# First chunks' normalized pairs in buffers of their own, gate weights at lower priority, and one v projection moved, in a two-layer decoder step

## The chip, the core and the metric

The kernel runs on one core of a Trainium2 chip. The metric is the device time of one execution in microseconds (us); lower is better. A measurement gives the median of several runs. Everything here is one program whose instructions are put in order, engine by engine, when it is built: a scheduler takes the code's steps with a priority each and decides which stands where in each engine's queue. At run time every engine works through its own queue strictly in that order.

## What is computed

A prompt of 2048 positions and a group of eight short samples go through two layers. Only the first layer matters here, and of it the beginning of the prompt:

```python
u = rmsnorm(h, norm_g)
proj = u @ w_in
q, k, v, gate, g_low = jnp.split(proj, [...], axis=-1)
log_a = jax.nn.log_sigmoid((g_low @ w_gate2 + b_gate)) / A_GATE_NORMALIZER
o, state = gla_recurrence(q, k, v, log_a, state0)      # per head, in chunks
o = rmsnorm(o, out_norm_g)
return (o * jax.nn.silu(gate)) @ w_out, state
```

There are four heads with 128 key columns and 512 value columns each; the gate that decides how fast the state decays comes from a projection of rank 16 (`g_low`).

## The kernel before

**Blocks and chunks.** The prompt is cut into 4 blocks of 512 positions, and each block into 4 chunks of 128. The work goes head by head and, in a head, block by block (`blocks`, line 936): 16 stretches, one for each. Every float32 operand is carried as a pair of float16 numbers, a high and a low piece, and a product takes three passes (`PASSES`): high by high, high by low, low by high.

**Normalizing the input.** `u_steps(j)` (line 374) loads block j's x in four chunks, two halves each, and calls `norm_T` (line 298) for each chunk. That squares and sums on ACT (for the first block the second half on DVE), takes the inverse root on POOL (`rsqrt`, line 183), writes the scaled high piece on ACT and the low piece on DVE into two tiles `xt` (line 310), and sends each tile by a transposing DMA from SP's queue into `uT[j]`. The tiles have the tag `ogT` with two buffers, so one chunk's pair takes both. The same tag serves the spills of the layer's output (`spill_og`, line 620).

**The start.** The program loads the first block's x and the first head's q and k weights, then calls `split_wg` (line 335), five operations on POOL that scale the low-rank gate weights and lay them out as pairs, then loads the first head's v weights (`hw[0].v.steps()`): eight pieces of 256 KB, each split on ACT and DVE. `qk_first` (line 443) projects q and k of the first block chunk by chunk as the chunks arrive; `glow` projects the low-rank gate; `logs` turns it into the running log decay `bt`. Then comes the second block's x, and the first head's gate weights.

**The first stretch.** A `weave` at line 937 issues the projections of v of the first block's four chunks and of the gate of its first chunk (`vg_steps`, line 464; 24 matmuls of 512 columns for each v or gate of a chunk), with the decay levels as fill. The levels (`level_steps`, line 484) build the matrix of decayed scores within a chunk: a diagonal and seven levels, each a few operations on DVE, ACT and POOL, twelve small matmuls into the one `lev` bank and a masked copy on DVE. `decay_steps` makes `qe`, `ke` and `Sh` from them, in tags with `NG` = 2 buffers. In the code of each block that follows, `chunk_steps(c)` (line 566) updates the state and reads it out, woven with the projections of the next chunk (line 983), and with the levels of the next block. In the first block's own stretch also block 2's x is normalized, in the second block's stretch block 3's.

**Priorities.** `behind(steps, n)` (line 174) lowers the priority of steps by n, so that the scheduler takes them only when other work is not ready. In the second block's stretch POOL also prepares rope tables (`rope_table`, line 890), through tiles that go out to memory again.

Of the kernel before, what the change touches and what calls it, by code (L numbers as in the profile page):

```python
# [10 lines left out]
F16 = mybir.dt.float16  # L11
# [8 lines left out]
P = 128  # L20
D = 1024
# [53 lines left out]
def _body(tc, nc, cp, sb, ps, dr, i, o):  # L75
    uniq = [0]

    def nm(s):
        uniq[0] += 1
        return f"{s}_{uniq[0]}"  # L80

    def T(tag, shape, dt, bufs=None):
        return sb.tile(shape, dt, tag=tag, name=nm(tag), **({} if bufs is None else {"bufs": bufs}))
# [67 lines left out]
    def weave(main, fill):  # L151

        main, fill = list(main), list(fill)
        done = 0
        for n, f in enumerate(main):
            f()
            upto = len(fill) * (n + 1) // len(main)
            for g in fill[done:upto]:
                g()
            done = upto  # L160
        for g in fill[done:]:
            g()

    def run(steps):
        for f in steps:
            f()

    def mix(a, b):

        out = []  # L170
        weave([lambda f=f: out.append(f) for f in a], [lambda f=f: out.append(f) for f in b])
        return out

    def behind(steps, n):


        def one(f):
            with tc.high_priority(offset=-n):
                f()

        return [lambda f=f: one(f) for f in steps]

    def rsqrt(ss, n, a, b, k=1, r=None):
        m = T("rs_m", [P, 8], F32, 4)
        r = T("rs_r", [P, 8], F32, 6) if r is None else r
        pool.tensor_scalar(m[:n, :k], ss, a, b, ALU.mult, ALU.add)  # L186
        pool.tensor_tensor(r[:n, :k], m[:n, :k], mhalf[:n, :k], ALU.pow)  # L187
        return r
# [106 lines left out]

        return [lambda part=todo[x : x + per]: step(part) for x in range(0, len(todo), per)], box

    def norm_T(xh, n, dst, both=False, flat=False):

        junk = T("og", [P, 512], BF16, 1)  # L300
        ss = T("ss", [P, 3], F32, 4)
        act(junk[:n], xh[0], AF.Square, accum_out=ss[:n, 0:1])
        if both:
            junk = T("S", [P, 512], F32, 1)
            dve.tensor_tensor_reduce(junk, xh[1], xh[1], 1.0, 0.0, ALU.mult, ALU.add, ss[:, 1:2])
        else:
            act(junk[:n], xh[1], AF.Square, accum_out=ss[:n, 1:2])
        dve.tensor_tensor(ss[:n, 2:3], ss[:n, 0:1], ss[:n, 1:2], ALU.add)
        r = rsqrt(ss[:n, 2:3], n, 1.0 / D / SU / SU, EPS / SU / SU)
        xt = [T("ogT", [P, D], F16, 2) for _ in range(2)]  # L310
        for half in range(2):
            cs = slice(half * 512, half * 512 + 512)
            if both is None:
                pool.tensor_scalar(xh[half], xh[half], r[:n, 0:1], None, ALU.mult)
                split((xt[0][:n, cs], xt[1][:n, cs]), xh[half], eng=pool)
            else:
                split((xt[0][:n, cs], xt[1][:n, cs]), xh[half], r[:n, 0:1])
        for hl in range(2):
            if flat:
                nc.sync.dma_start(dst(hl), xt[hl][:n])  # L320
            else:
                nc.sync.dma_start(dst(hl), xt[hl][:n], transpose=True)

    uT = [T("uT", [P, KT, 2, 512], F16, 4) for _ in range(NBL)]
# [10 lines left out]
    def split_wg():  # L335
        pool.tensor_tensor(wg_raw, wg_raw, gs_a.unsqueeze(2).to_broadcast([P, KT, RANK]), ALU.mult)
        pool.tensor_copy(wg[:, :, :RANK], wg_raw)
        pool.tensor_tensor(wg[:, :, RANK : 2 * RANK], wg_raw, wg[:, :, :RANK], ALU.subtract)
        for n in range(1, 3):
            pool.tensor_copy(wg[:, :, n * 2 * RANK : (n + 1) * 2 * RANK], wg[:, :, : 2 * RANK])  # L340
# [33 lines left out]
    def u_steps(j):  # L374
        def chunk(c):
            if j > 0:
                t = T("W", [P, D], F32, NW)
                xh = [t[:, :512], t[:, 512:]]
            else:
                xh = [T("v", [P, 512], F32, 4) if c > 1 else T(tag, [P, 512], F32, 2) for tag in ("st", "sth")]  # L380
            for half in range(2):
                nc.sync.dma_start(xh[half], i["x_prompt"][0, j * 512 + c * P : j * 512 + (c + 1) * P, half * 512 : half * 512 + 512])
            norm_T(xh, P, lambda hl: uT[j][:, :, hl, c * P : (c + 1) * P], j == 0)

        return behind([lambda c=c: chunk(c) for c in range(4)], 20 if j > 0 else 0)

# [497 lines left out]
    def some(n=2):  # L884
        out = prep[:n]
        del prep[:n]
        return out
# [18 lines left out]
    cur = Blk(0, 0, hw[0])  # L906
# [1 line left out]
    first = u_steps(0)  # L908
    qkw = [f for u in hw[0].qk for f in u.steps()]
    run([first[0]] + qkw[:2] + [first[1]] + qkw[2:] + first[2:4])  # L910
    split_wg()
    run(hw[0].v.steps())
    load_w2()
    bgate = C("bgate", [P, 2 * AH], F32)
# [6 lines left out]
    f = T("pst", [P, 7, 64], F32, 2)  # L921
# [12 lines left out]
            wo1.units[u].t = t[:, u]  # L934

    blocks = [(h, j) for h in range(AH) for j in range(NBL)]
    weave([f for c in range(4) for f in cur.vg_steps(c, (0,))] + cur.vg_steps(0, (1,)), cur.level_steps() + cur.decay_steps())
    prev_tail = []
    samp = None
    sparts = []  # L940

    for n, (h, j) in enumerate(blocks):
# [9 lines left out]
        lv = nxt.level_steps() if nxt else []  # L952
# [13 lines left out]
        if last:  # L966
            ch = [cur.chunk_steps(c) for c in range(3)]
            weave([f for c in range(1, 4) for f in cur.vg_steps(c, (0,))], ch[0] + lv[:3] + ch[1][:3] + lv[3:5] + ch[2][:3])
            run(hw[h + 1].v.steps() if h + 1 < AH else wo.steps()[4:])
            for c in range(1, 4):  # L970
                weave(cur.vg_steps(c, (1,)), (ch[c - 1][3:] if c > 1 else []) + lv[3 + c * 2 : 5 + c * 2])
            for f in ch[2][3:]:
                f()
            run(hw[h + 1].g.steps() if h + 1 < AH else wo1.steps()[8:])
        else:
            for c in range(3):
                if n == len(blocks) - 2:
                    if c == 0:
                        wo_aside()
                    more = (wo1.steps()[:8] + wo.steps()[:4])[c * 4 : c * 4 + 4]  # L980
                else:
                    more = side[c * 2 : c * 2 + 2] if n < 2 else some(PR[j])
                weave(cur.vg_steps(c + 1, (0, 1) if n else (1,)), mix(cur.chunk_steps(c) + lv[(0,3,6)[c]:(3,6,8)[c]], sparts[(0,3,7)[c]:(3,7,99)[c]]) + more)
                if j == NBL - 2 and h + 1 < AH and c == 0:
                    hw[h + 1] = head_weights(h + 1)
                    for u in hw[h + 1].qk:
                        for f in u.steps():
                            f()
            sparts = []
# [53 lines left out]
        if j == NBL - 1:  # L1043
            sparts = samp.steps()
# [4 lines left out]
        cur = nxt  # L1049
# [636 lines left out]
    for t in range(-3, NKV * NCH):  # L1686
        fill = []
        n = t + 3
        if n < NKV * NCH:
            g, c = divmod(n, NCH)  # L1690
# [59 lines left out]
    for p_ in range(NCH // 2):  # L1750
        more = []
        if p_ + 1 < NCH // 2:
            nxt = pairs[p_ + 1]
            ld, sm = [lambda x=x, nxt=nxt: nxt.load(x) for x in (2, 3, 0, 1)], nxt.sums()
            more = ld[:2] + sm[:2] + ld[2:3] + sm[2:6]
# [88 lines left out]
```

## Time and profile before

| | us |
|---|---|
| median of 3 runs | 2862.69 |
| lowest, highest | 2857.28, 2869.30 |
| the profiled execution | 2863.85 |
| its span, first to last instruction | 2862.1 |

The profile shows one execution. PE is TensorE, DVE VectorE, ACT ScalarE, POOL GpSimd, SP the engine whose queue issues most DMAs (SPq in rows). Times in it count from the span's start. A row of a timeline gives start, length, engine, line, operation, output and inputs, how many instructions were merged and, in brackets, how long the engine was idle before and what ended that.

[...] The first hundred microseconds stand out in the profile's second part: PE is at 60% in the first of 40 slices and at 80% in the second, and at 90% or more in nearly all others.

### The profile page before, as it was taken

The numbers are of one execution on the slowest core, as the hardware profiler recorded it, in microseconds if no ns is written. First come the engines' busy times: TensorE is split into PE (matmuls) and PEld (weight loads), VectorE is DVE, ScalarE is ACT, GpSimd is POOL, SyncE is SP. The second block draws the span as 40 slices with busy tenths as digits, with TensorE's granted clock in tenths as the row PEclk, the third lists the DMA queues.
The fourth block names the chain that finished last, engine by engine and source line by source line (L and its number), as shares of the span: only waits on it lengthen the run. The fifth ranks groups of instructions, "written<-read, shape, count | busy, mean of one in ns | idle before, by whom it ended". The sixth has DMA issues, their size and how long they took to land.

```text
span 2862.1 us, 51609 instructions
## 1 busy us (share of the span) xinstructions
PE 2735.9 (96%) x19070; PEld 1392.4 (49%) x19070; DVE 1845.7 (64%) x3815; ACT 1440.3 (50%) x3385; POOL 1063.6 (37%) x1471
## 2 busy tenths in 40 slices
PE   6899999999999999999899999999999999988999
PEld 3445444444454444444344555555555555543444
DVE  5767787677768775336413666677777766767653
ACT  6655665466546654333313555566666666641110
POOL 1242233222322321116405676666566556530000
PEclk9899999999999999999999999999999999999999
DMA  8351334124312533799975555866877788798651
GB/s 209 90 124 36 100 101 150 38 82 136 115 38 85 171 84 96 180 240 282 233 193 135 108 130 120 203 117 129 173 116 130 157 155 165 151 236 172 125 112 57
DMA packets 774230, 391.78 MB, mean 137 GB/s; under 512 B 629200, under 2 KB 698776, under 8 KB 773944
## 3 DMA queue, kind: packets, MB, share of 16 engines
q1 hardware_dynamic: 761016, 352.75, 54.6%
q0 software_dynamic: 10880, 35.66, 3.4%
q8 instruction: 149, 2.44, 0.4%
q14 instruction: 105, 0.86, 0.1%
q10 hardware_dynamic: 2080, 0.07, 0.0%
HBM read 138.90 MB, written 107.54 MB: 86 GB/s over the span
## 4 chain that ended last, share of the span: by engine, by line
PE 56%; DVE 12%; DMA 11%; ACT 10%; issue 6%; POOL 4%; SPq 1%; DVEq 0%; ACTq 0%; POOLq 0%
PE pj L101 33%; PE o L101 11%; PE tr L101 8%; PE kv L101 3%; ACT o L1279 2%; DMA pst<-v 2%; DVE v L198 2%; ACT v L197 2%; DMA pre<-pst 1%; PE lev L101 1%; DMA wraw<-in_a_w_in_dram 1%; DVE o L1274 1%; DVE W L198 1%; POOL ogT L195 1%; DVE lev L1274 1%
## 5 line engine op out<-in xcount | busy, mean ns | idle before, releaser
L101 PE MATMUL pj<-W,uT 128*128 128x512 f16 x5088 | 1208.1, 383 | 6.6 <-ACT qT L430 2.9
L101 PEld LDWEIGHTS <-uT 128*128 128x128 f16 x6976 | 654.7, 99 | 714.1 <-issue 40.4
L101 PE MATMUL tr<-W,uT 128*128 128x512 f16 x1536 | 365.8, 379 | 0.0
L186 POOL TENSOR_SCALAR rs_m<-ss 128x1 f32<-128x1 f32 (+3 forms) x190 | 46.1, 243 | 685.7 <-ACT og L611 234.0
L101 PEld LDWEIGHTS <-X 128*128 128x128 f16 x2744 | 185.8, 98 | 149.3 <-issue 14.7
L1279 ACT ACTIVATE o<-o,mx 128x256 f32<-128x256 f32 (+1 forms) x384 | 168.5, 439 | 168.1 <-DVE mx L1274 163.6
L1274 DVE CUSTOM_DVE_ANT_0 o<-o,madd,nsink 128x256 f32<-128x256 f32 (+1 forms) x384 | 184.0, 479 | 48.3 <-PE o L101 44.0
L101 PE MATMUL pj<-uT,W 128*128 128x512 f16 (+1 forms) x912 | 186.0, 354 | 27.0 <-DMA uT<-ogT 24.3
L198 DVE SCALAR_TENSOR_TENSOR v<-o,v 128x512 f16<-128x512 f32 (+1 forms) x192 | 128.8, 671 | 102.0 <-ACT v L197 82.0
L187 POOL TENSOR_TENSOR rs_r<-rs_m,mhalf 128x1 f32<-128x1 f32 (+2 forms) x186 | 184.8, 994 | 14.4
L101 PEld LDWEIGHTS <-W 128*128 128x128 f16 x2448 | 128.0, 98 | 113.1 <-issue 18.5
L101 PEld LDWEIGHTS <-v 128*128 128x128 f16 x976 | 95.2, 98 | 116.0 <-DMA v<-ogd 1.9
L508 POOL TENSOR_TENSOR E<-bt 128x256 f32<-128x256 f32 x96 | 73.9, 770 | 198.4 <-DVE X L195 124.8
L195 POOL TENSOR_TENSOR ogT<-og,ogT 128x512 f16<-128x512 f32 x68 | 88.0, 1295 | 154.4 <-ACT ogT L194 142.5
L101 PEld LDWEIGHTS <-sth 128*128 128x128 f16 x2080 | 111.4, 99 | 52.3 <-DMA sth<-v 12.2
L101 PEld LDWEIGHTS <-sg 128*128 128x128 f16 x800 | 78.6, 99 | 107.5 <-DMA sg<-ogd 12.3
L101 PE MATMUL o<-gl,X 128*128 128x256 f16 (+1 forms) x768 | 114.9, 273 | 5.5 <-DMA X<-qe 5.5
L197 ACT ACTIVATE v<-o 128x512 f16<-128x512 f32 (+1 forms) x192 | 111.3, 579 | 11.1 <-DMA sth<-v 7.6
L101 PE MATMUL kv<-rmask,sth 128*128 128x64 f16 x1984 | 107.0, 194 | 10.1 <-DMA sth<-v 9.2
L101 PE MATMUL kv<-rmask,pst 128*128 128x64 f16 x992 | 102.4, 194 | 9.3 <-DMA pst<-v 9.3
L1279 ACT ACTIVATE lev<-lev,mx 128x256 f32<-128x256 f32 (+1 forms) x128 | 56.5, 441 | 103.3 <-DVE mx L1274 101.2
L101 PE MATMUL pj<-W,v 128*128 128x512 f16 x448 | 104.2, 379 | 1.1 <-DMA v<-ogd 1.1
(468 smaller groups left out, 5092.5 us busy)
## 6 DMA issues: line engine op xcount, KB each, us to landing
pre<-pst POOLq DMA_DIRECT2D x72, 256.0 KB, 3.4
W<-pre SPq DMA_DIRECT2D x36, 512.0 KB
ogd<-ogT SPq DMA_DIRECT2D x68, 256.0 KB
wraw<-in_a_w_in_dram SPq DMA_DIRECT2D x64, 256.0 KB
wraw<-in_b_w_in_dram SPq DMA_DIRECT2D x64, 256.0 KB
oge<-ogT SPq DMA_DIRECT2D x64, 256.0 KB
wraw<-in_a_w_out_dram SPq DMA_DIRECT2D x32, 256.0 KB
X<-in_x_prompt_dram SPq DMA_DIRECT2D x32, 256.0 KB
```

Of the source, the lines that this page charges most:

```text
L101: return order(nc.tensor.matmul(*a, **k))
L186: pool.tensor_scalar(m[:n, :k], ss, a, b, ALU.mult, ALU.add)
L187: pool.tensor_tensor(r[:n, :k], m[:n, :k], mhalf[:n, :k], ALU.pow)
L195: eng.tensor_tensor(lo, src, hi, ALU.subtract)
L197: act(hi, src, AF.Copy, scale=sc)
L198: dve.scalar_tensor_tensor(lo, src, sc, hi, ALU.mult, ALU.subtract)
L508: pool.tensor_tensor(Ev[:, :, 0, :], ref, btv[:, :, 0, :], ALU.subtract)
L1274: dve.tensor_tensor_reduce(pm[:, z], pm[:, z], madd.rearrange("p a b -> p (a b)")[:, (2 - nk) * P :], -0.125, nsink[:, g * GRP + h : g * G ...
L1279: act(pm[:, z], pm[:, z], AF.Exp, scale=-1.0, bias=nm_[:, h : h + 1], accum_out=bx["sum"][:, h : h + 1])
```

## The change

There are three edits. The pairs of the first block's four chunks get a tag each, `ogT`, `qe`, `ke` and `Sh`, whose tiles have the same size and are first used for their own purpose later. `split_wg` runs at a priority lower by 400. And v of the first block's fourth chunk is no longer projected in the first `weave` but in the first block's stretch, with that chunk's gate.

```diff
--- before.py
+++ after.py
@@ -295,7 +295,7 @@
 
         return [lambda part=todo[x : x + per]: step(part) for x in range(0, len(todo), per)], box
 
-    def norm_T(xh, n, dst, both=False, flat=False):
+    def norm_T(xh, n, dst, both=False, flat=False, tag="ogT"):
 
         junk = T("og", [P, 512], BF16, 1)
         ss = T("ss", [P, 3], F32, 4)
@@ -307,7 +307,7 @@
             act(junk[:n], xh[1], AF.Square, accum_out=ss[:n, 1:2])
         dve.tensor_tensor(ss[:n, 2:3], ss[:n, 0:1], ss[:n, 1:2], ALU.add)
         r = rsqrt(ss[:n, 2:3], n, 1.0 / D / SU / SU, EPS / SU / SU)
-        xt = [T("ogT", [P, D], F16, 2) for _ in range(2)]
+        xt = [T(tag, [P, D], F16, 2) for _ in range(2)]
         for half in range(2):
             cs = slice(half * 512, half * 512 + 512)
             if both is None:
@@ -380,7 +380,7 @@
                 xh = [T("v", [P, 512], F32, 4) if c > 1 else T(tag, [P, 512], F32, 2) for tag in ("st", "sth")]
             for half in range(2):
                 nc.sync.dma_start(xh[half], i["x_prompt"][0, j * 512 + c * P : j * 512 + (c + 1) * P, half * 512 : half * 512 + 512])
-            norm_T(xh, P, lambda hl: uT[j][:, :, hl, c * P : (c + 1) * P], j == 0)
+            norm_T(xh, P, lambda hl: uT[j][:, :, hl, c * P : (c + 1) * P], j == 0, tag="ogT" if j > 0 else ("ogT", "qe", "ke", "Sh")[c])
 
         return behind([lambda c=c: chunk(c) for c in range(4)], 20 if j > 0 else 0)
 
@@ -908,7 +908,7 @@
     first = u_steps(0)
     qkw = [f for u in hw[0].qk for f in u.steps()]
     run([first[0]] + qkw[:2] + [first[1]] + qkw[2:] + first[2:4])
-    split_wg()
+    run(behind([split_wg], 400))
     run(hw[0].v.steps())
     load_w2()
     bgate = C("bgate", [P, 2 * AH], F32)
@@ -934,7 +934,7 @@
             wo1.units[u].t = t[:, u]
 
     blocks = [(h, j) for h in range(AH) for j in range(NBL)]
-    weave([f for c in range(4) for f in cur.vg_steps(c, (0,))] + cur.vg_steps(0, (1,)), cur.level_steps() + cur.decay_steps())
+    weave([f for c in range(3) for f in cur.vg_steps(c, (0,))] + cur.vg_steps(0, (1,)), cur.level_steps() + cur.decay_steps())
     prev_tail = []
     samp = None
     sparts = []
@@ -980,7 +980,7 @@
                     more = (wo1.steps()[:8] + wo.steps()[:4])[c * 4 : c * 4 + 4]
                 else:
                     more = side[c * 2 : c * 2 + 2] if n < 2 else some(PR[j])
-                weave(cur.vg_steps(c + 1, (0, 1) if n else (1,)), mix(cur.chunk_steps(c) + lv[(0,3,6)[c]:(3,6,8)[c]], sparts[(0,3,7)[c]:(3,7,99)[c]]) + more)
+                weave(cur.vg_steps(c + 1, (0, 1) if n or c == 2 else (1,)), mix(cur.chunk_steps(c) + lv[(0,3,6)[c]:(3,6,8)[c]], sparts[(0,3,7)[c]:(3,7,99)[c]]) + more)
                 if j == NBL - 2 and h + 1 < AH and c == 0:
                     hw[h + 1] = head_weights(h + 1)
                     for u in hw[h + 1].qk:
```

The scheduler's order changes with it on every engine, in the first three blocks of the first head; behind that the orders of all engines agree. Three places follow.

SP's queue at the start, as it was. A `wraw` is a piece of weights that comes in, a `DMA_TRANSPOSE` sends one piece of a chunk's pair (first the high, then the low one) into `uT_156`, the first block's; `ogT_256` and 257 are the second chunk's, 293 and 294 the third's, 315 and 316 the fourth's.

```order
L322 DMA_TRANSPOSE uT_156<-ogT_256 128x8x128
L322 DMA_TRANSPOSE uT_156<-ogT_257 128x8x128
L223 DMA wraw_347<-in_a_w_in_dram 128x512
L223 DMA wraw_351<-in_a_w_in_dram 128x512
L223 DMA wraw_356<-in_a_w_in_dram 128x512
L322 DMA_TRANSPOSE uT_156<-ogT_293 128x8x128
L322 DMA_TRANSPOSE uT_156<-ogT_294 128x8x128
L223 DMA wraw_360<-in_a_w_in_dram 128x512
L108 DMA pst_364<-in_a_w_gate_dram 16x512 x3
L322 DMA_TRANSPOSE uT_156<-ogT_315 128x8x128
L322 DMA_TRANSPOSE uT_156<-ogT_316 128x8x128
```

And with the change:

```order
L223 DMA wraw_338<-in_a_w_in_dram 128x512
L322 DMA_TRANSPOSE uT_156<-qe_256 128x8x128
L223 DMA wraw_342<-in_a_w_in_dram 128x512
L322 DMA_TRANSPOSE uT_156<-qe_257 128x8x128
L322 DMA_TRANSPOSE uT_156<-ke_293 128x8x128
L223 DMA wraw_347<-in_a_w_in_dram 128x512
L322 DMA_TRANSPOSE uT_156<-Sh_315 128x8x128
L322 DMA_TRANSPOSE uT_156<-ke_294 128x8x128
L322 DMA_TRANSPOSE uT_156<-Sh_316 128x8x128
L223 DMA wraw_351<-in_a_w_in_dram 128x512
L223 DMA wraw_356<-in_a_w_in_dram 128x512
L223 DMA wraw_360<-in_a_w_in_dram 128x512
```

The transfers of chunks two to four have moved together: one load of weights stands between the second chunk's last and the fourth chunk's last, where there were four, and the low-rank gate's second weights (`pst_364`) now follow all of them.

ACT at the first block's first level, before. `v_…` is a chunk's v split, `X_748` the diagonal's split and `X_778` level 0's, `E` a decay factor, and the `ogT` are the second block's chunks.

```order
L197 ACTIVATE ogT_654<-W_642,rs_r_651 128x512 x2
L197 ACTIVATE X_748<-E_746 128x512
L197 ACTIVATE v_940<-pj_869 128x512
L510 ACT_TABLE_LOAD
L510 ACTIVATE E_772<-E_772 128x512
L197 ACTIVATE ogT_674<-W_662,rs_r_671 128x512 x2
L197 ACTIVATE v_1013<-pj_943 128x512
L194 ACTIVATE X_778<-E_772 128x512
L510 ACTIVATE E_808<-E_808 128x512
```

And with the change:

```order
L197 ACTIVATE v_963<-pj_892 128x512
L197 ACTIVATE ogT_654<-W_642,rs_r_651 128x512
L197 ACTIVATE X_744<-E_742 128x512
L197 ACTIVATE ogT_654<-W_642,rs_r_651 128x512
L510 ACT_TABLE_LOAD
L510 ACTIVATE E_769<-E_769 128x512
L477 ACTIVATE sg_1030<-pj_988 128x512
L197 ACTIVATE ogT_674<-W_662,rs_r_671 128x512 x2
L194 ACTIVATE X_775<-E_769 128x512
```

There is one v split less; the third chunk's v is done ahead of the diagonal, and the first chunk's gate (`sg_1030`) has moved ahead of level 0. On PE, level 0 now stands whole ahead of the second block's q and k, where the gate of the first chunk stood.

POOL in the second block's stretch, before. `pst` are rope tables, `rs_m` and `rs_r` the two steps of an inverse root, `ogT_1860` the low piece of a spill.

```order
L897 TENSOR_TENSOR pst_2666<-pst_2666,gq 128x512
L186 TENSOR_SCALAR rs_m_1852<-ss_1850 128x1
L897 TENSOR_TENSOR pst_2673<-pst_2673,gq 128x512
L901 DMA rtd<-pst_2666 128x8x64
L187 TENSOR_TENSOR rs_r_1853<-rs_m_1852,mhalf 128x1
L901 DMA rtd<-pst_2673 128x8x64
L195 TENSOR_TENSOR ogT_1860<-og_1849,ogT_1860 128x512
L899 TENSOR_TENSOR pst_2857<-pst_2857,gq 128x8x32
L900 TENSOR_TENSOR pst_2857<-pst_2857,gq 128x8x32
L186 TENSOR_SCALAR rs_m_1959<-ss_1955 128x1
```

And with the change:

```order
L897 TENSOR_TENSOR pst_2666<-pst_2666,gq 128x512
L897 TENSOR_TENSOR pst_2673<-pst_2673,gq 128x512
L901 DMA rtd<-pst_2666 128x8x64
L901 DMA rtd<-pst_2673 128x8x64
L186 TENSOR_SCALAR rs_m_1852<-ss_1850 128x1
L187 TENSOR_TENSOR rs_r_1853<-rs_m_1852,mhalf 128x1
L899 TENSOR_TENSOR pst_2857<-pst_2857,gq 128x8x32
L900 TENSOR_TENSOR pst_2857<-pst_2857,gq 128x8x32
L899 TENSOR_TENSOR pst_2865<-pst_2865,gq 128x8x32
L900 TENSOR_TENSOR pst_2865<-pst_2865,gq 128x8x32
L901 DMA rtd<-pst_2857 128x8x64
L195 TENSOR_TENSOR ogT_1860<-og_1849,ogT_1860 128x512
```

Both rope tables now go ahead of the first root, and four operations of the next two ahead of the spill. POOL's operations up to the first block's levels, `split_wg`'s among them, stand in the order in which they stood.

## Rows read from the trace of the kernel before

**Rows 1.** The page's first part: busy time, share of the span and instructions of each engine.

```profile
PE 2735.9 (96%) x19070; PEld 1392.4 (49%) x19070; DVE 1845.7 (64%) x3815; ACT 1440.3 (50%) x3385; POOL 1063.6 (37%) x1471
```

**Rows 2.** Busy time by stretch of 100 us: engine, instructions, granted clock, DMA share, GB/s.

```profile
0.00:100.00 100.00, 71.65 (x508) 41.43 (x509) 61.80 (x120) 60.54 (x108) 20.15 (x45) 0.93 0.69 163
100.00:200.00 100.00, 88.39 (x497) 41.63 (x496) 72.34 (x136) 59.39 (x121) 42.34 (x62) 0.93 0.54 124
```

**Rows 3.** Timeline of PE, 17 to 50 us: start, length, instructions, idle time and releaser.

```profile
23.82 2.73 PE L101 MATMUL pj<-uT,W 128*128 128x128 f16 x46 [0.34 <-DMA uT<-ogT]
...
30.32 4.21 PE L101 MATMUL pj<-uT,W 128*128 128x128 f16 x48 [0.58 <-DMA uT<-ogT]
...
35.41 2.73 PE L101 MATMUL pj<-uT,W 128*128 128x128 f16 x46 [0.66 <-DMA uT<-ogT]
37.97 3.40 PE L101 MATMUL tr<-uT,ogTs 128*96 128x512 f16 x15
41.21 6.21 PE L101 MATMUL pj<-W,uT 128*128 128x512 f16 x28
```

**Rows 4.** Timeline of the other engines and of SP's queue, 8 to 34 us.

```profile
8.38 1.01 POOL L340 COPY ogTs<-ogTs 128x256 f16<-128x256 f16 x2
...
9.48 0.24 POOL L186 TENSOR_SCALAR rs_m<-ss 128x1 f32<-128x1 f32 x1
...
22.90 1.33 ACT L197 ACTIVATE ogT<-v,rs_r 128x512 f16<-128x512 f32 x2 [0.42 <-DMA uT<-ogT]
...
24.26 2.63 SPq L322 DMA_TRANSPOSE uT<-ogT  x2
...
29.53 1.33 ACT L197 ACTIVATE ogT<-v,rs_r 128x512 f16<-128x512 f32 x2 [1.81 <-DMA uT<-ogT]
...
30.89 2.62 SPq L322 DMA_TRANSPOSE uT<-ogT  x2
```

**Rows 5.** DMA queue's share, 95 to 103 us (one transfer), and a stretch of plain loads.

```profile
q1 hardware_dynamic: 1056, 0.26, 17.1%
...
40.00:47.00 7.00, 7.00 (x34) 3.25 (x33) 2.71 (x4) 2.35 (x5) 0.00 (x0) 1.00 1.02 374
```

**Rows 6.** Timeline of ACT at 47 us, and the stretch behind it.

```profile
47.15 0.63 ACT L307 ACTIVATE og<-W 128x512 bf16<-128x512 f32 x1 [3.70 <-DMA W<-in_x_prompt_dram]
...
48.00:52.00 4.00, 4.00 (x20) 1.77 (x19) 2.76 (x6) 4.00 (x9) 0.74 (x2) 1.00 0.24 67
```

**Rows 7.** Timeline of PE, 65 to 145 us; between its rows one split on DVE.

```profile
65.47 0.33 PE L101 MATMUL lev<-one_h,X 128*128 128x1 f16 x7 [2.19 <-DVE X L198]
66.06 7.03 PE L101 MATMUL pj<-W,uT 128*128 128x512 f16 x24 [0.27 <-DVE v L198]
...
69.90 0.68 DVE L198 SCALAR_TENSOR_TENSOR v<-pj,v 128x512 f16<-128x512 f32 x1
...
92.79 7.94 PE L101 MATMUL pj<-W,uT 128*128 128x512 f16 x24 [0.35 <-ACT qT L430]
...
95.00:97.00 2.00, 2.00 (x6) 0.62 (x5) 1.24 (x3) 1.98 (x4) 0.00 (x0) 0.50 0.00 0
...
136.19 0.80 PE L101 MATMUL lev<-X 128*128 128x64 f16 x12 [5.29 <-ACT X L194]
138.64 2.85 PE L101 MATMUL pj<-uT,W 128*128 128x512 f16 x6 [1.65 <-DMA uT<-ogT]
```

**Rows 8.** Timeline of the second block's end: DVE, POOL and PE.

```profile
161.54 1.12 POOL L901 DMA_DIRECT2D rtd<-pst  x1
...
163.29 0.75 DVE L614 SCALAR_TENSOR_TENSOR og<-o,rs_r,sg 128x512 f32<-128x512 f32 x1 [6.26 <-POOL rs_r L187]
...
164.79 1.15 POOL L195 TENSOR_TENSOR ogT<-og,ogT 128x512 f16<-128x512 f32 x1 [0.66 <-ACT ogT L194]
...
179.02 0.18 PE L101 MATMUL lev<-one_h,X 128*128 128x1 f16 x1 [3.71 <-ACT X L197]
179.60 5.30 PE L101 MATMUL pj<-W,uT 128*128 128x512 f16 x16 [0.40 <-DVE sg L478]
```

## Prediction

> **What bounds the kernel now.** I read the page's busy shares first, then the stretches of 100 us, then PE's timeline through the first two of them, then the timelines of the other engines at PE's waits. PE is busy for 96% of the span [rows 1], so little is left anywhere; what is left stands at the start: PE works 71.65 us of the first hundred and 88.39 of the second [rows 2]. The change touches only work issued in those two. The reader should see four waits there.
>
> First, the start. The four chunks of the first block share one pair of `ogT` buffers, so a chunk can be written only when the one ahead has left by its two transposing transfers: ACT's passes at 22.90 and 29.53 start after waits for just that [rows 4], and PE gets its chunks at 23.82, 30.32 and 35.41 [rows 3]. Behind the fourth chunk come 46 matmuls and 15 of the low-rank gate, and at 41.21 the projection of v.
>
> Second, the wait of 2.19 us at 65.47 for the split of the first block's diagonal, a DVE matter, and the slow matmuls behind it [rows 7]. Third, the waits of 5.29 and 1.65 us ahead of the third block's q and k [rows 7]. Fourth, the 3.71 us at 179.02, for the diagonal of the block after [rows 8].
>
> **Own buffers: the start.** Nothing is computed that was not before; the tags `qe`, `ke` and `Sh` have two buffers of the same size each, not used until long after. What goes is the wait for the pair. One transfer of 0.26 MB alone on the queue takes 17.1% of 8 us, 1.37 us of all sixteen engines [rows 5]; SP needs 2.62 us to issue two [rows 4]. Between the second chunk's landing (23.82) and the fourth's (35.41) lie 11.6 us, in which the four transfers need only 5.5. A plain load of 256 KB takes 0.70 us at 374 GB/s [rows 5]; in the new order one load of v weights stands between the four transfers, and three that stood there go behind. So the last landing comes at 23.8 + 5.5 + 0.7 = 30.0 instead of 35.4. PE can use only part of it: the third chunk's second piece is the last transfer but one, 28.6, and 48 matmuls take 2.73 us at full clock and 4.21 where the clock had fallen during a wait [rows 3]. The fourth chunk's turn then comes at 31.3 to 32.8; it was 35.41. I take the middle: **3.4 us earlier**. Bounds: 0, if the queue is full anyway, and 5.4, the landing's whole gain. From there the 61 matmuls follow as now, and the v weights put behind (three loads, 2.1 us, and a split) land by 34, ahead of their use.
>
> Does the gain pass on? ACT's next wait is 3.70 us for the second block's x at 47.15, then it is busy 4.00 us of 4.00 [rows 6]. Those loads are issued behind the same transfers on SP, so they come earlier by the same; the chain by ACT and DVE to the levels moves along with PE.
>
> So a transposing transfer takes 1.37 us where a plain one takes 0.70 [rows 5]. [...]
>
> **Gate weights behind.** POOL prepares them in five operations that end at 9.39, and the first chunk's norm starts on POOL at 9.48 [rows 4]: it queues behind them. But POOL's order is, up to the first block's levels, row for row what it was: at 6 us nothing else was ready for the scheduler to take. This part costs 0 and brings 0. Had it moved, at most 2 us of the first chunk could follow; the bounds are both 0 because the order is known.
>
> **The fourth chunk's v.** 24 matmuls, at 6.21 us for 28 some 5.3 us [rows 3], and one split on each of ACT and DVE (0.68 us on DVE [rows 7]) leave the stretch ahead of the levels and come back in the first block's. In the old place PE loses cover: it already waited 2.19 us there, and now reaches the first block's diagonal and level by some 5 us earlier than they can be ready, since these hang on ACT and DVE. The wait itself sets nothing back. [...] In the new place the 5.3 us lie inside the 5.29 + 1.65 us in which PE waits; but the split stands on DVE ahead of the chain of norms and transfers that ends the second of these, 0.7. Together **1.6 us later**; bounds 0 and 7.7 (1.7, 0.7 and all 5.3 us uncovered).
>
> **What the scheduler moves with it.** In the second block POOL's rope tables move ahead of a norm and of a spill, and the third block's decay chain (gate split, scan) moves ahead of that norm on DVE. Before, DVE sat 6.26 us for POOL's root with that chain queued behind [rows 8]. The norm now has one more 1.12 us issue ahead of it; the chain is free; but `ogT_1860`, 1.15 us on POOL, is put behind four rope operations, and ACT's next squares need its buffer. What can be won is PE's 3.71 us and the slow start behind it, 16 matmuls in 5.30 us instead of 3.6 [rows 8]: 5.4 in all. I take **1.5 us earlier**; bounds 5.4 earlier and 1.1 later. Behind some 300 us the orders of all engines agree again, and nothing there has changed but its start.
>
> **Sum.** 3.4 − 1.6 + 1.5 = 3.3 us less. The profiled execution took 2863.85 us with a span of 2862.1, so 2860.5; it stands 1.2 above the median of the runs (2862.69), so as a median 2859.4 us, 0.12% less.
>
> **Rivals.**
> *The moved v is not hidden* (slower). It decides at the third block's q and k: PE's waits there are 6.94 us, the moved work 5.3, so if the transfers come more than 1.6 us earlier relative to PE than now, the matmuls begin to set the end. All of it uncovered, with the slow clock: −3.4 + 1.7 + 0.7 + 5.3 = 4.3 later, less nothing in the block after: 2867. For it: that margin is thin. Against it: the transfers there still share one pair of buffers. [...]
>
> *The change does not do what it says* (no change). The gate weights have not moved, and the transfers may only queue up: between 23.82 and 35.41 the four transfers and four v loads need 5.5 + 2.8 = 8.3 of 11.6 us. If the loads keep their share, the fourth chunk gains 3.3 us at landing, of which the third chunk's matmuls leave PE about 1; the other terms cancel: 2861.7.
>
> *All gaps close* (faster). With v in the gap PE no longer waits 6.94 us at 131 to 139, the clock stays up, and the 5.4 us at 179 go too: 5.4 + 5.4 and some 1.2 of clock, 12 us, 2850.7. Against it: the waits end by ACT, DVE and transfers, not by PE's want of work.
>
> **How the numbers follow.** Forecast 0.5, not hidden 0.17, no effect 0.2, all gaps close 0.13. The range takes in all four, with a margin of about 2 us for the runs' own scatter (2857.28 to 2869.3): 2849 to 2868. A measurement can tell about 0.5% from no change, 14.3 us, and no case here reaches that; faster 0.06 and slower 0.02 stand for what I have not seen, the faster side larger because some 30 us of waits and slow clock lie in the first two hundred.
>
> **What would show it.** Right: ACT's passes of chunks 2 to 4 no longer wait for `uT`; the last chunk's matmuls start near 31 to 33; v's projection at 38; the wait ahead of level 0 grows to about 5 us; the one at 136 shrinks below 2; POOL's copies still end at 9.4; the third block's q and k start near 137. Wrong: the last landing at 34 or later, or PE without a wait ahead of the third block's q and k, which would mean that v is exposed; or a difference between the traces behind 300 us.

## The result, and the profile after

The changed kernel takes 2869.54 us, the median of 20 runs (2863.36 to 2884.22), the kernel before, timed beside it, 2863.09 (20 runs, 2855.1 to 2872.51). The ratio is 1.0027, with a 95% interval of 1.0017 to 1.0037: 6.5 us slower by the medians, 7.7 by the ratio, 5 to 11 by the interval. That is within the 0.5% that I had called the same, but on the other side of no change and just above my range (2849 to 2868). The profiled execution took 2868.72 us, with a span of 2866.9.

The page's busy shares, of the kernel after:

```profile
PE 2730.4 (95%) x19070; PEld 1390.1 (48%) x19070; DVE 1847.2 (64%) x3815; ACT 1438.0 (50%) x3385; POOL 1069.0 (37%) x1471
```

Its busy time by stretch (columns as in [rows 2]):

```profile
0.00:100.00 100.00, 67.49 (x486) 39.59 (x487) 62.30 (x119) 58.02 (x106) 20.83 (x45) 0.90 0.67 163
100.00:200.00 100.00, 85.38 (x466) 39.00 (x465) 70.15 (x130) 55.95 (x113) 42.40 (x56) 0.91 0.51 119
60.00:70.00 10.00, 2.65 (x25) 1.38 (x24) 8.94 (x17) 6.08 (x10) 3.87 (x5) 0.64 0.81 180
70.00:80.00 10.00, 9.02 (x30) 4.07 (x31) 5.43 (x12) 2.89 (x5) 4.79 (x9) 0.68 0.42 107
```

PE does 4.2 us less in the first hundred and 3.0 less in the second [rows 2], at a lower granted clock in both (0.90 and 0.91, where both had 0.93; 1.00 is full speed). The two short stretches, for the kernel before:

```profile
60.00:70.00 10.00, 7.54 (x37) 3.21 (x35) 9.08 (x17) 8.28 (x15) 2.88 (x4) 0.87 0.66 152
70.00:80.00 10.00, 10.00 (x67) 5.24 (x66) 6.70 (x14) 3.72 (x7) 5.76 (x10) 0.96 0.59 140
```

PE's timeline of the kernel after, at the places that the prediction named:

```profile
28.49 7.04 PE L101 MATMUL pj<-uT,W 128*128 128x128 f16 x94 [0.41 <-DMA uT<-ke]
35.36 3.40 PE L101 MATMUL tr<-uT,ogTs 128*96 128x512 f16 x15
38.60 3.62 PE L101 MATMUL pj<-W,uT 128*128 128x512 f16 x16
...
67.53 0.23 PE L101 MATMUL lev<-X 128*128 128x64 f16 x1 [3.97 <-ACT X L194]
69.14 0.75 PE L101 MATMUL lev<-X 128*128 128x64 f16 x11 [1.38 <-DVE X L195]
70.98 0.58 PE L101 MATMUL pj<-uT,W 128*128 128x512 f16 x1 [1.09 <-DMA uT<-ogT]
...
71.79 3.62 PE L101 MATMUL pj<-uT,W 128*128 128x512 f16 x8
...
88.40 0.51 PE L101 MATMUL lev<-X 128*128 128x64 f16 x12
...
140.54 0.38 PE L101 MATMUL pj<-uT,W 128*128 128x512 f16 x1 [2.57 <-DVE S L531]
141.37 4.83 PE L101 MATMUL pj<-uT,W 128*128 128x512 f16 x14 [0.45 <-DMA uT<-ogT]
...
181.30 0.18 PE L101 MATMUL lev<-one_h,X 128*128 128x1 f16 x1 [4.52 <-ACT X L197]
...
188.72 6.55 PE L101 MATMUL pj<-W,uT 128*128 128x512 f16 x21 [4.47 <-DVE sg L478]
```

The start is won: the v projection begins at 38.60 instead of 41.21 [rows 3]. The second block's q and k begin at 70.98, 2.0 us earlier than before (72.96), but 8 matmuls of them take 3.62 us; when all of them are done, at the level at 88.40, PE is 0.4 us late (that level stood at 88.01). Ahead of them PE waits 3.97 and 1.38 us for ACT and DVE at level 0 and 1.09 us for the transfers. The third block's q and k begin at 140.54 instead of 138.64 [rows 7]: 1.9 late. Then come 4.52 and 4.47 us of waits where there were 3.71 and 0.40 [rows 8], and the projection of the sample, 160 small matmuls, begins at 291.81 instead of 283.30: 8.5 late. So the loss was 2.4 us at 71 to 88, 1.5 by 141 and 6.6 behind it, against 2.6 won at the start and 0.6 of it gone by 71.

What became of the gain between v and 71 us stands in ACT's rows: the split of the first block's diagonal, and the pass that writes the second block's last chunk. Before:

```profile
62.41 0.61 ACT L197 ACTIVATE X<-E 128x512 f16<-128x512 f32 x1
...
66.41 1.33 ACT L197 ACTIVATE ogT<-W,rs_r 128x512 f16<-128x512 f32 x2 [0.92 <-DVE E L511]
```

And in the kernel after:

```profile
60.08 0.61 ACT L197 ACTIVATE X<-E 128x512 f16<-128x512 f32 x1
...
65.62 1.33 ACT L197 ACTIVATE ogT<-W,rs_r 128x512 f16<-128x512 f32 x2 [1.89 <-DMA uT<-ogT]
```

The chain to the levels is 2.3 us earlier, the last chunk only 0.8: it now waits 1.89 us until the chunk ahead of it has left, as the second block's chunks still share one pair of buffers.

The largest piece, in the timeline of the kernel after, POOL's rows first and ACT's behind them:

```profile
163.90 2.02 POOL L901 DMA_DIRECT2D rtd<-pst  x2
165.94 0.20 POOL L186 TENSOR_SCALAR rs_m<-ss 128x1 f32<-128x1 f32 x1
166.22 0.56 POOL L187 TENSOR_TENSOR rs_r<-rs_m,mhalf 128x1 f32<-128x1 f32 x1
170.09 0.72 POOL L899 TENSOR_TENSOR pst<-pst,gq 128x256 f32<-128x256 f32 x1 [3.31 <-DMA pst<-in_c_rope_dram]
170.77 0.72 POOL L900 TENSOR_TENSOR pst<-pst,gq 128x256 f32<-128x256 f32 x1
173.36 1.13 POOL L899 TENSOR_TENSOR pst<-pst,gq 128x256 f32<-128x256 f32 x1 [1.87 <-DMA pst<-in_c_rope_dram]
174.46 1.17 POOL L900 TENSOR_TENSOR pst<-pst,gq 128x256 f32<-128x256 f32 x1
...
176.55 1.16 POOL L195 TENSOR_TENSOR ogT<-og,ogT 128x512 f16<-128x512 f32 x1
...
163.12 0.19 ACT L611 ACTIVATION_READ_ACCUMULATOR og<-o 128x1 f32 x1
...
167.60 0.63 ACT L194 ACTIVATE ogT<-og 128x512 f16<-128x512 f32 x1 [4.29 <-DVE og L614]
...
177.75 0.63 ACT L302 ACTIVATE og<-W 128x512 bf16<-128x512 f32 x1 [5.75 <-POOL ogT L195]
...
180.63 0.61 ACT L197 ACTIVATE X<-E 128x512 f16<-128x512 f32 x1
```

POOL's half of the spill (`ogT<-og`, line 195) could start when ACT's half ended, at 168.2. It starts at 176.55, because four rope-table operations stand ahead of it in POOL's order, and two of them wait for their loads, 3.31 and 1.87 us (the first of these waits began at 166.78, ahead of 168.2). The spill's input is itself late: the norm's root could start at 163.3, when ACT had its sum, and starts at 165.94, behind the two tables that now go first and their two issues. The squares of the next norm need the spill's `og` buffer: ACT waits 5.75 us. The split of the diagonal stands behind the squares on ACT (180.63), and PE waits for that, 4.52 us. The tanh and the gate behind it come late too: 4.47 more.

### The profile page after: what moved, and what is told of

Read it like the earlier page. It is cut to its first block, busy times and chain, and to the rows that moved or that the text cites. A ratio compares the mean times of both kernels' runs of the same rounds, so it can differ in the third digit from the quotient of the medians.

```text
span 2866.9 us, 51619 instructions
## 1 busy us (share of the span) xinstructions
PE 2730.4 (95%) x19070; PEld 1390.1 (48%) x19070; DVE 1847.2 (64%) x3815; ACT 1438.0 (50%) x3385; POOL 1069.0 (37%) x1471
## 4 chain that ended last, share of the span: by engine, by line
PE 55%; DVE 12%; DMA 12%; ACT 10%; issue 7%; POOL 4%; SPq 1%; DVEq 0%; ACTq 0%; POOLq 0%
PE pj L101 32%; PE o L101 11%; PE tr L101 8%; PE kv L101 3%; ACT o L1279 2%; DMA pst<-v 2%; DVE v L198 2%; DMA pre<-pst 2%; ACT v L197 2%; PE lev L101 1%; DMA wraw<-in_a_w_in_dram 1%; DVE o L1274 1%; DMA uT<-ogT 1%; DVE W L198 1%; POOL ogT L195 1%
```

## The experiments

Thirteen runs in four sets, each timed against the kernel before on the same chip (median there 2858.3 to 2860.1). The sets ran on different chips, so ratios are compared and not times; a forecast in us below is meant beside 2863.1 where it names no other time. "v", "q,k 2", "q,k 3" and "sample" are starts on PE, in us, in the profiled execution.

| kernel | ratio (95%) | v | q,k 2 | q,k 3 | sample |
|---|---|---|---|---|---|
| before | 1 | 41.2 | 73.0 | 138.6 | 283.3 |
| the change | 1.0027 (1.0017 to 1.0037) | 38.6 | 71.0 | 140.5 | 291.8 |
| 1 own buffers | 1.0021 (1.0011 to 1.0030) | 37.7 | 73.7 | 143.0 | 287.6 |
| 2 v moved | 1.0026 (1.0014 to 1.0037) | 40.4 | 71.5 | 140.5 | 288.6 |
| 3 the change, spill first | 0.9998 (0.9987 to 1.0008) | 39.3 | 70.6 | 139.1 | 281.8 |
| 4 own buffers, v moved | 1.0034 (1.0023 to 1.0046) | 36.4 | 74.5 | 141.5 | 291.6 |
| 5 before, spill first | 0.9994 (0.9980 to 1.0008) | 40.6 | 72.3 | 137.3 | 276.4 |
| 6 v moved, spill first | 1.0008 (0.9993 to 1.0022) | 40.8 | 71.4 | 140.3 | 283.5 |
| 7 run 3 with added matmuls | 0.9969 (0.9954 to 0.9984) | 38.1 | 72.1 | 134.0 | 279.0 |
| 8 run 3 with v back | 1.0009 (0.9994 to 1.0024) | 36.9 | 68.4 | 138.2 | 285.6 |
| 9 the change with added matmuls | 0.9997 (0.9986 to 1.0008) | 36.8 | 70.8 | 134.3 | 285.2 |
| 10 run 6 with added matmuls | 1.0000 (0.9988 to 1.0013) | 40.3 | 71.6 | 140.0 | 285.1 |
| 11 run 5 with added matmuls | 1.0002 (0.9991 to 1.0014) | 40.1 | 75.6 | 141.4 | 289.1 |
| 12 gate weights' place | 1.0002 (0.9987 to 1.0016) | 40.9 | 71.7 | 137.0 | 281.5 |
| 13 run 3, second order on ACT | 1.0004 (0.9991 to 1.0017) | 36.9 | 70.5 | 136.0 | 281.5 |

Run 12 has the kernel before's order on PE and POOL, row for row, and starts the sample 1.8 us earlier. The change and runs 3, 7, 8, 9 and 13 have one order on all engines up to v, and v stands between 36.8 and 39.3 in them. So one profile's place is good to 2 or 2.5 us.

**Runs 1 and 2: one part each.** Run 1 is the change's `tag` in `norm_T` and in `u_steps`; run 2 its two lines in the weaving of `vg_steps`.

> Own buffers alone, nothing else of the change. Theory (the loss lies in the third block's stretch, where POOL's spill of the second block's gated output stands behind rope-table work that waits for its loads): in this kernel's order the spill stands ahead of that work, and the start still gains 2.6 us at the first v projection (38.6 instead of 41.2), so 2857 to 2862, 1 to 6 us under the kernel before. Rival one (the moved v is exposed): the same sign, 2859 to 2862. Rival two (own buffers themselves cost the time, by pushing v's weight loads behind): 2866 or more, and a v projection at 40 or later.

> The fourth chunk's v moved, alone; the four chunks keep one pair of buffers. Its POOL order in the third block's stretch is the changed kernel's: the spill behind four rope operations. Theory: the whole loss of that stretch is here too (a wait of 4 to 5 us at the block's diagonal and one of 4 us behind it), so 2867 to 2872. Rival one (the moved v is exposed): 2867 to 2872 as well, but PE then reaches the third block's q and k without a wait for the transfers. Rival two (own buffers cost the time): 2861 to 2864.

Run 1 missed: it is 0.21% slower. The spill stands ahead of the four rope operations, but not of the two tables before them: ACT's half ends at 161.58 and POOL's starts at 165.43. Still, from the third block's q and k to the sample run 1 takes 144.6 us and the kernel before 144.7, so its loss lies ahead of that. Its timeline, a row of DVE and one of PE:

```profile
50.59 1.22 DVE L372 TENSOR_TENSOR_SCAN bt<-rmask,E 128x512 f32<-128x512 bf16 x1
...
73.72 0.58 PE L101 MATMUL pj<-uT,W 128*128 128x512 f16 x1 [5.97 <-DMA uT<-ogT]
```

PE is 3.5 us ahead at v, but here the first block's decay chain (its scan at 50.59; 58.00 in the kernel after) has moved ahead of the second block's norms. The levels are done early, and the norms are late: ACT writes the second block's last chunk at 68.48 (66.41 before). PE waits 5.97 us for the transfers, and starts q and k 0.8 later than before. No run puts this order back, so that it is the cause of run 1's loss is not shown. Rival two has the sign and not the mechanism, as v's projection is early. Run 2 came as the theory said, with PE waiting ahead of the third block's q and k (2.76 and 0.72 us), so the moved v is covered there. The theory of one loss did not hold; there is a second, at the second block's q and k. Each part alone costs about as much as the whole, so the parts' losses don't add.

**Run 3: the order on POOL.** All rows up to the third block's stretch stay those of the changed kernel.

```diff
+            x = eng.tensor_tensor(lo, src, hi, ALU.subtract)
+            if eng is pool:
+                spills.append(x)
...
+        def aft(x):
+            tc.add_manual_dep(x.ins, spills[4].ins.name, ...)
...
+            aft(pool.tensor_tensor(t, t, g.to_broadcast([P, N2, HD]), ALU.mult))
```

> The changed kernel whole, with one thing more: POOL's rope-table work may not stand ahead of that one spill (an order on POOL alone; the same instructions). All rows up to the third block's stretch are the changed kernel's. Theory: the waits of 4.5 us at that block's diagonal and 4.5 us behind it shrink to the kernel before's 3.7 and 0.4 or less, so 4 to 7 us less than the changed kernel's 2869.5: 2862 to 2866, level with the kernel before. Rivals one and two: it stays at 2868 to 2871, since neither the moved v nor the buffers' order is touched.

It is level with the kernel before, as forecast: 8 us less than the change (1.0027 to 0.9998). Its timeline, rows of POOL, ACT and PE (the added lines shift the line numbers by 2 to 4):

```profile
163.65 1.16 POOL L197 TENSOR_TENSOR ogT<-og,ogT 128x512 f16<-128x512 f32 x1 [1.53 <-ACT ogT L196]
...
164.84 0.63 ACT L306 ACTIVATE og<-W 128x512 bf16<-128x512 f32 x1 [0.76 <-POOL ogT L197]
...
176.46 0.33 PE L101 MATMUL lev<-one_h,X 128*128 128x1 f16 x7 [0.49 <-DVE X L202]
177.05 5.34 PE L101 MATMUL pj<-W,uT 128*128 128x512 f16 x24 [0.27 <-DVE sg L482]
```

The squares start 12.9 us earlier, and the waits of 4.52 and 4.47 us are 0.49 and 0.27. Of the 12.9, 8.2 are the spill's, 2.5 the root's, which no longer stands behind the two tables (the edit holds these back as well), and some 2 us stood already ahead of both, where the orders are still the same. This takes the change's loss away; run 5 asks how much of the 8 us is a gain of the edit's own.

**Run 4: without the gate weights' edit.** Own buffers and the moved v.

> Own buffers and the moved v, gate weights prepared where they were. The spill stands behind two of the four rope operations in the third block's stretch, not four. Theory: the spill waits for one load instead of two, so some 3 of the 6 us lost there come back: 2864 to 2868. Rival one: 2868 to 2871, as the moved v is the same. Rival two: 2868 to 2871 as well.

Above the theory's range and the rivals': a ratio of 1.0034 is 2873 us beside 2863.1. With the spill behind two operations the stretch from the third block's q and k to the sample takes 150.1 us, against 151.3 in the change, so little comes back; and PE waits 9.07 us for the second block's transfers, which here come at 74.48.

**Runs 5, 6 and 8: the order on POOL beside other parts.** Run 5 is the third run's edit on the kernel before, run 6 on run 2; run 8 is run 3 with v's two lines undone.

> The kernel before with the order of the third run alone (POOL's rope-table work not ahead of that one spill), nothing of the change. It asks whether the 9 us that the order took off the changed kernel are damage undone or a gain of its own. Theory (there are both: the kernel before also waits 3.7 us at the third block's diagonal, and 16 slow matmuls follow): 3 to 6 us less than the kernel before, ratio 0.998 to 0.999; then the rest of the change, on equal terms, costs 2 to 5 us. Rival (the order only undoes what the change did): within 1 us of the kernel before, and the rest of the change is worth nothing or a little.

> The moved v alone with the same order on POOL. Theory: the waits at the third block's diagonal and behind it go as they did with the whole change, 6 to 9 us less than the moved v alone (2868.2 beside 2859.6): 2859 to 2862 beside 2859.6. If so, own buffers are worth less than 2 us beside the third run. Rival (the moved v is exposed): no change from the moved v alone.

> The changed kernel with the order on POOL and the fourth chunk's v back in its old place: only this move is undone beside the third run. Theory: in its old place v keeps PE busy ahead of the second block's q and k, so the start's 2.6 us are passed on there (no slow clock); in exchange the 5 us of waits ahead of the third block's q and k come back. The two about cancel: within 2 us of the third run. Rival (the moved v is exposed): 3 to 5 us less than the third run.

In run 5 the waits at the third block's diagonal are gone, and the sample starts 6.9 us earlier; the ratio, 0.9994, leaves 2 us of that, with an interval that reaches from 6 us less to 2 more. That is less than the theory's 3 to 6 us and more than the rival's 1. So the order is mostly damage undone, with a gain of its own that the runs don't settle. Run 6 gets back 5 of run 2's 7.4 us, a little less than the 6 to 9 expected. With the spill in its place, the change's other parts cost 0.0004 (run 3 against run 5), less than the intervals tell. Run 8 is 3 us slower than run 3 (the intervals overlap), not 3 to 5 faster: the moved v is not what costs. The theory's mechanism missed as well: PE waits 3.33 us ahead of the second block's q and k there too, and 7 matmuls behind that take 3.17 us.

**Runs 7, 9, 10 and 11: matmuls that nobody reads.** Run 7 is run 3 with matmuls into unused columns of the level's PSUM tile, in the first block's level 0 alone; 9, 10 and 11 are the same on the change and on runs 6 and 5.

```diff
                 pl = PT("lev", [P, 512])
+                def warm(n):
+                    if self.h == 0 and self.j == 0 and li == 0:
+                        for _ in range(n):
+                            mm(pl[:, 256:512], idh, uT[0][:, 0, 0, :256], start=True, stop=True)
+                warm(28)
...
+                warm(16)
                 dve.copy_predicated(
```

> The third run's kernel with 28 matmuls of 256 columns ahead of the first block's level 0 and 16 behind it; they write columns of a PSUM tile that nothing reads, so they are work added for nothing, in PE's wait there. Theory on the second loss (what the start gained goes, because PE then waits 7 us for the second block's transfers and works on its q and k at the half clock): the granted clock from 70 to 80 us rises from 0.80 (0.68 in the changed kernel) to over 0.95, the second block's q and k end 1 to 2 us earlier (the level that stands at 78.9 comes at 77 to 78), and the whole is 0 to 2 us less. Rival (the clock falls for another reason, or the transfers alone set those matmuls): no earlier, and the added 3 to 5 us show in the whole, 2 to 5 us more.

> The changed kernel with the added matmuls of the seventh run and without the order on POOL: the fourth corner beside the changed kernel, the third run and the seventh. In this kernel's order the spill stands behind two of the four rope operations. Theory (two losses that add): the slow clock at the second block's q and k is gone (granted clock over 0.95 from 70 to 80 us), the third block's waits stay in part, so between the changed kernel's ratio of 1.0027 and the seventh run's 0.9969: 0.998 to 1.001. Rival (the seventh run's gain is all from the added matmuls, the order on POOL is worth nothing beside them): 0.996 to 0.998.

> The seventh run without the own buffers and without the gate weights' place: the moved v, the order on POOL and the added matmuls. Theory: what the own buffers gain at the start (2 to 3 us) is passed on once PE's clock holds, so this is 2 to 4 us more than the seventh run: a ratio of 0.9975 to 0.999. Rival (own buffers are worth nothing, since the second block's transfers set its q and k): the seventh run's 0.997 within 0.0005.

> The kernel before with the order on POOL and the same added matmuls. Here the fourth chunk's v still stands ahead, so PE has no long wait at level 0 and the added matmuls come in its way. Theory (they help only where PE would wait and lose its clock): 2 to 6 us more than the fifth run's 0.9994: 1.000 to 1.0015, and the second block's q and k start 3 us later than in the fifth run. Rival (the added matmuls help by the order that the scheduler makes with them, not by the clock): less than the fifth run, 0.996 to 0.9985.

Run 7 is 0.31% faster than the kernel before and beats both kernels; 8 us less than run 3 is more than the 0 to 2 forecast. Its profiled execution is the fastest of its twelve (2843.51 us; median 2850.90), so its places lean early. Its busy time from 70 to 80 us:

```profile
70.00:80.00 10.00, 10.00 (x77) 6.11 (x76) 6.18 (x12) 3.13 (x6) 4.58 (x9) 1.00 0.24 79
```

and the same stretch of run 3:

```profile
70.00:80.00 10.00, 9.41 (x47) 4.57 (x48) 6.31 (x13) 3.35 (x6) 5.06 (x9) 0.80 0.35 96
```

PE's timeline of run 7 (the 28 matmuls are the first of the added ones):

```profile
64.32 5.86 PE L101 MATMUL lev<-uT,idh 128*128 128x256 f16 x28 [1.93 <-DVE S L502]
...
72.55 1.89 PE L101 MATMUL pj<-uT,W 128*128 128x512 f16 x8
...
133.97 0.38 PE L101 MATMUL pj<-uT,W 128*128 128x512 f16 x1 [1.39 <-DVE X L197]
```

The granted clock is 1.00, where run 3 had 0.80 and the change 0.68 (0.50 from 71 to 76 us); 8 matmuls take 1.89 us instead of the change's 3.62. From 60 to 70 us PE was busy for 6.39 us in run 7, for 2.51 in run 3 and for 2.65 in the change, at 0.66, 0.69 and 0.64. So in these kernels the slow clock from 70 to 80 us comes with that wait. Of run 3's wait only 0.80 us is for the transfers; 4.02 and 1.37 us are for ACT and DVE at level 0, which the expectation above counts in with them.

But the gain is not mainly that. The added matmuls end at 72.1, 1.5 us behind run 3's start of q and k, and when q and k are done run 7 is 0.1 ahead. It is 5.1 ahead at the third block's q and k. Run 9 gains the same (134.31 against 140.54), run 10 nearly nothing there (139.96 against 140.25), though its clock is up as well, as its row shows:

```profile
70.00:80.00 10.00, 10.00 (x79) 6.62 (x78) 4.87 (x11) 2.49 (x5) 4.88 (x10) 0.95 0.42 110
```

So a clock of 0.95 there does not by itself bring that start. What runs 7 and 9 share there and run 10 lacks is an order on ACT. Run 7, the first block's gate ahead of the second block's diagonal:

```profile
98.58 0.60 ACT L481 ACTIVATE sg<-pj 128x512 f32<-128x512 f32 x1
...
99.87 0.63 ACT L201 ACTIVATE X<-E 128x512 f16<-128x512 f32 x1
```

In run 10, as in the change (101.47 and 104.53), this split comes first (101.50), and the gate behind it (104.64). Run 11, where nothing had to be held, starts the second block's q and k 3.3 us later than run 5, as expected, and the third block's 4 us later. Runs 9 and 11 fell in the theory's range; run 10 just above it (0.9975 to 0.999).

**Run 12: the gate weights' place.**

> The gate weights' place alone. PE's and POOL's orders are those of the kernel before, row for row; only a load moves on SP's queue and rows on ACT and DVE at the start. All theories: no difference, a ratio of 0.999 to 1.001, and a first v projection within 0.5 us of 41.2. A time over 1.002 would put part of the loss on this edit.

As expected: no difference that the interval tells. In the change the edit is not without effect on the orders: without it the spill stands behind two rope operations instead of four (run 4).

**Run 13: what stands behind run 7's 5 us.** In run 7 four ACT instructions of the first block's stretch have the kernel before's order again. Run 13 sets this order by itself:

```diff
+                        y = act(s, box[0], AF.Tanh, scale=0.5 * DESC)
+                        if (self.h, self.j, c) == (0, 0, 1):
+                            for a, b in zip([y] + held, held):
+                                tc.add_manual_dep(b.ins, a.ins.name, ...)
```

(`held` is the square, the split and the exponential.)

> The third run's kernel (the change, POOL's spill first) with one order more, on ACT and with no added matmuls: the first block's gate of chunk 1 (a tanh), the square of chunk 0's output, the diagonal's split and the first level's exponential of the second block, in this sequence, which is the kernel before's and the seventh run's; the changed kernel and the third run have them as split, square, exponential, tanh, with a table load of 1.28 us on the way. Theory (the 5 us that the seventh run has at the third block's q and k come from this order, since the spill and the norm's squares behind it start 2.6 us earlier, and not from the clock): the squares start near 104 us (106.65 in the third run), the third block's q and k at 134 to 136 (139.09; 133.97 in the seventh), and the whole is 2 to 6 us less than the kernel before: a ratio of 0.998 to 0.9993. Rival (the added matmuls did it by holding the clock): the third run's 139 and 0.9998, within 0.0006.

The timeline of run 13, ACT's square and then PE:

```profile
105.15 0.61 ACT L307 ACTIVATE og<-W 128x512 bf16<-128x512 f32 x1
...
136.04 0.38 PE L101 MATMUL pj<-uT,W 128*128 128x512 f16 x1 [2.48 <-DVE X L197]
...
186.76 1.01 PE L101 MATMUL kv<-v,ke 128*128 128x512 f16 x2 [3.79 <-DVE v L202]
```

The square comes 1.5 us earlier than run 3's and the third block's q and k 3.1 us earlier, so the order is a cause there, and the added matmuls are not needed for it (though 3.1 us is not far above what one profile's place is good to). The whole is no faster: 1.0004, against a forecast of 0.998 to 0.9993. Behind 136 stands a new wait of 3.79 us at 186.76, and the sample starts at 281.5, where run 3 has 281.8. Why run 7 keeps its gain is therefore open. 2.8 us of its 8 stand at the sample's start; the rest lies behind it, where PE's and SP's orders are equal. From 1300 to 1500 us the transfers run at a share of 0.89 to 0.95, and PE's work there differs from profile to profile (185.57 to 192.05 us). Busy time by stretch of run 7:

```profile
1300.00:1500.00 200.00, 192.05 (x1099) 89.95 (x1098) 73.83 (x95) 53.46 (x106) 65.65 (x88) 0.97 0.90 227
```

and of run 5:

```profile
1300.00:1500.00 200.00, 185.57 (x1068) 86.63 (x1066) 74.13 (x96) 51.80 (x104) 66.47 (x90) 0.97 0.92 224
```

That is 6.5 us more work in the same 200 us, between two kernels whose program is the same there. Over the whole, run 5's profile is 2.6 us ahead of run 7's at the sample and 8.5 behind it at the end (spans of 2850.2 and 2841.7 us).

## Why the prediction was wrong

**Own buffers: nearly right at the start, wrong in what follows.** I forecast 3.4 us; v's projection came 2.6 earlier, within the bounds, and ACT's passes of the later chunks no longer wait for `uT`. The landing came as computed (the third chunk's last piece at 28.49, forecast 28.6); of the two prices for the 48 matmuls behind it the slow one held: 94 matmuls took 7.04 us, of which 46 at full clock are 2.73 (granted clock 0.78 from 28.40 to 36.00; the slow price is from 30.30 to 34.60 in the kernel before, at 0.66, behind a wait of 2.91 us). What failed here is the passing on, "the chain by ACT and DVE to the levels moves along with PE". The chain moved, by 2.3 us, but the second block's transfers did not move with it: for this block I had left out that its chunks still share one pair of buffers, and the last one is written only 0.8 us earlier. PE, reaching the second block's q and k early, waits for level 0 and then for these transfers, and then works at a lower clock (0.68 from 70 to 80 us; 0.96 before).

**Gate weights: right by itself.** POOL's copies end at 9.30 (9.39 before), and run 12 finds no difference.

**The fourth chunk's v: the cover right, the price too low.** I took 1.6 us. Between v's projection and the third block's q and k the kernel lost 4.5 (from 2.6 early to 1.9 late), inside my bounds of 0 to 7.7. The wait ahead of level 0 grew to 5.35 us, as I had said. Of my 1.6 us 0.9 were for a slow clock behind that wait, with a bound of 1.7 (24 matmuls in 7.03 us [rows 7] less 5.3); no run shows the 0.9. What the runs showed in its place is the larger part of 2.4 us between 71 and 88: 8 matmuls in 3.62 us in the change and in 1.89 in run 7, at a granted clock of 1.00, are 1.7. The rival of the uncovered v forecast 2867, the nearest of the four, but by the wrong mechanism: PE still waits 3.0 us ahead of the third block's q and k, and run 8 gives no sign that v is better back. Of that rival's sum only the 1.7 us of slow clock came true. The 1.5 us between 88 and 141 I did not have at all. ACT's order had changed there, and run 13, which sets it right, has 3.1 us less than run 3; a loss of 1.5 is itself within what one profile's place is good to.

**What the scheduler moves: wrong in sign, and its bound wrong too.** This is the step of the prediction that failed most. I forecast 1.5 us won, between 5.4 won and 1.1 lost; it lost 6.6. Of the 11.8 us between my 3.3 won and the 8.5 lost at the sample, 8.1 are here, 2.9 at the moved v and 0.8 at the start. I had the very row, "`ogT_1860`, 1.15 us on POOL, is put behind four rope operations, and ACT's next squares need its buffer", and gave it no price: the bound of 1.1 is the norm's one issue of 1.12 us. The four operations take 3.7 us and wait for loads, 3.31 and 1.87 us, and the spill came 8.3 us after its input was ready. The norm's root, for which that issue was the price, came 2.6 us late. Run 3 takes this step away, and with it the whole loss; by run 5 some 2 us of these 8 may be the edit's own gain (its interval on the kernel before: 6 us less to 2 more).

**What would show it.** As forecast: v at 38 (38.60), the wait at level 0 (5.35), POOL's copies, and no wait left at the level at 136. Not: the third block's q and k at 137 (140.54), ahead of which 3.0 us of waits stand. Behind 300 us the orders agree, as said; between the profiles the sample's 8.5 us shrink to 4.8 at the end, within what kernels with equal orders differ there (runs 5 and 7: 11 us).

## What to carry to other kernels

Where a scheduler orders the queues, a small edit at the start can reorder instructions a hundred microseconds later. Look through those rows as closely as the edit: an operation put behind others in an engine's queue can take on their waits for loads, not just their lengths. Here a spill of 1.16 us on POOL stood behind operations of 3.7 us and waits of 3.31 and 1.87, and came 8.3 us after its input was ready. One dependency that keeps it in place took the change's whole loss off (8 us; on the kernel before it was worth some 2, within its interval). And time won ahead of a wait that doesn't move with it is not won: here it became idle time of PE (3.97, 1.38 and 1.09 us), with a granted clock of 0.68 behind it where 0.96 stood.

## What the runs showed of the hardware that I had not expected

Forty-four matmuls whose output nobody reads took the granted clock from 70 to 80 us from 0.80 to 1.00, and the kernel with them was the fastest of all here, though the same brought run 10 little (1.0000 against run 6's 1.0008). The same forty-four on the kernel whose PE did not have to wait there (run 11 against run 5) moved its q and k back by 3.3 us. And transposing transfers left on own buffers still took SP 1.23 to 1.75 us each to issue, one behind the other. From 20 to 28 us the sixteen DMA engines had a share of 1.16, so whether SP or these paced the row is not shown.
